# A hybrid DiT layer on one core: output projection by half token tiles, first MLP block in two halves, second norm without POOL, two hidden parts stored as hi and lo

## The chip, the core and the metric

The kernel runs on one core of one Trainium2 chip. A core has TensorE (PE: matrix products and transposes into the PSUM banks; its weight loads are shown as PEld), VectorE (DVE), ScalarE (ACT), GpSimd (POOL), SyncE (SP, which here only issues transfers), and transfer queues (DMA) between DRAM and the on-chip memory SBUF. Each engine works through its own instructions in order and waits on semaphores for the others. The metric is the device time of one execution in microseconds.

## The reference

One layer of a diffusion backbone on 1024 latent and 128 context tokens, `D_MODEL` 1024, everything in float32. What matters here is its second half:

```python
mix = (sigmoid(ga) * attn + sigmoid(gc) * conv) @ w_o
x = layer_norm(ALPHA * x + g1 * mix, ln1_g, ln1_b)
h = x * (1 + sc2) + sh2
f = square(relu(h @ w1 + b1)) @ w2 + b2
x = layer_norm(ALPHA * x + g2 * f, ln2_g, ln2_b)
```

`w_o` is 1024 x 1024, `w1` 1024 x 4096, `w2` 4096 x 1024. Shift, scale and gate (`sh2`, `sc2`, `g1`, `g2`) are rows, one set for the latent and one for the context tokens. Before that come the input projections, neighbourhood attention and a short convolution; the change leaves them alone.

## The kernel before

**Precision.** A float32 operand is cut into hi (a cast to the matrix format, on ACT) and lo (the difference, on DVE), and each product is three matmuls: hi x hi, hi x lo, lo x hi. So each operand costs one ACT cast and one DVE subtraction before PE can use it.

**Tokens** are 1152 columns: nine tiles of 128, three chunks of 384, or, for the MLP, two pairs of 576 (each two halves of `PT` = 288). Tile 4 lies across the two pairs.

**Order.** The program is written out by hand. Within one engine the order is that of the calls. `bg` is a list of small closures; `background(n)` (L705) calls the next n of them between groups of matmuls.

**Weights** of the projections come through `Ring` (L66 to L132): `load_to` issues the transfer of a 128 x 1024 raw tile (2 buffers) on SP, `split_hi` casts on ACT (L108), `split_lo` subtracts on DVE (L121) into one of 3 pairs of buffers; `take` returns the next pair and splits some ahead.

**Output projection** (L1150 to L1177). For each of three chunks, all eight 128-row blocks of `w_o` are streamed through the ring again (24 tiles of 512 KB). For each block, three token tiles accumulate into two PSUM banks each (`token_mm`, L990; six matmuls of 512 columns). At the end of a chunk `ln1_first` (L968) multiplies by the gate row (L974) and adds the residual (L975) for a whole tile; closures then take the moments (L981, L962 to L965), apply the norm on ACT (L985) and write the normalized tile to DRAM (`xd`, on ACT's queue, L986).

**Turning and modulating.** Normalized tiles are transposed on PE (L1043, L1058) and modulated by ACT on the way out of PSUM (L1033). For pair 0 `raw_four` does four tiles at once (512 columns), for pair 1 384 + 128. Pair 0 is done in the background of chunk 2; pair 1 after the projection has ended (L1189).

**First MLP product** (L1239 to L1319). It is a seven-product (Strassen-like) scheme over 16 blocks `j`: seven combinations of quarters of the tokens' matrix (`combine`, L1063: subtractions L1084, casts L1075, low parts L1079) meet seven combinations of quarters of `w1` (`w1_sum`, `w1_prep`, L1112 to L1146). `w1_mm` does both pairs, 24 matmuls of 288 columns for each of the seven. Results are kept on ACT (L1247) and added on DVE (L1250), then passed through relu and square, combined into seven hidden parts `B11 T1 T2 B21 T3 B22 T4` and written to DRAM as float32 (`spill`, L1235, on ACT's queue).

**Second MLP product** (L1590 to L1650). It runs through 7 products; the first five take both pairs in one step (24 matmuls, 80 steps), the last two (with `T4` and `B21`) one pair at a time (12 matmuls, 64 steps). `f2_load` (L1357) brings the weights and the hidden part seven steps ahead, `f2_prep` (L1388) cuts them three steps ahead (L1396 on ACT, L1399 on DVE).

**Second norm** (`ln2`, L1464) runs tile by tile (96 tokens) in the gaps of the last two products, from the list `side` with a credit per step (L1648). `residual` multiplies x by `ALPHA * ln1_g` on POOL (L1478), `o1` and `o2` transpose the result back and add it (L1486, L1491, L1492), `apply` normalizes on ACT (L1500), `gain` multiplies by a row on POOL (L1504), `last` adds a row on DVE (L1508). The last three tiles are ended by `end` (L1511) with work on ACT, POOL and DVE.

Of the kernel before, what the change touches and what calls it, by code (L numbers as in the profile page):

```python
# [18 lines left out]
P = 128  # L19
D = 1024  # L20
# [46 lines left out]
class Ring:  # L67
# [20 lines left out]
    def load_to(self, n):  # L88
        n = min(n, len(self.seq), self.nlo + self.raw_bufs + (1 if self.more else 0))
        while self.nload < n:  # L90
            ap, w = self.seq[self.nload]
            t = self.tile(F32, "wraw", self.nload, self.raw_bufs, "r")
            self.nc.sync.dma_start(t[:, :w], ap)
            self.raw[self.nload] = t
            self.nload += 1
# [48 lines left out]
def emit(nc, tc, ctx, aps, outs):  # L144
# [43 lines left out]
    for c in range(NCH):  # L188
        seq += [(aps["wo"][k], 1024) for k in range(KB)]
# [746 lines left out]
    sx0, sraw, sln, sw = ExitStack(), ExitStack(), ExitStack(), ExitStack()  # L936
    wsp = pool_on(sw, "wsp", side="right")
    hx0 = pool_on(sx0, "hx0", side="right")
    rawp = pool_on(sraw, "rawp", side="right")
# [13 lines left out]
    grow = [row(lnp, f"g{cond}", modd[cond, 0:D]) for cond in range(2)]  # L953
    xks = {}

    def load_xk(t):
        xks[t] = lnp.tile([P, D], F32, name=f"xk{t}")
        dma(xks[t], aps["xk"][t])
# [9 lines left out]
    def ln1_first(t, ps):  # L968

        x = xks[t]  # L970
        r = tmp(lnp, [P, D], "lnt", 1)
        g = grow[1 if t == 8 else 0]
        for i in range(2):
            vec.tensor_tensor(out=r[:, HALVES[i]], in0=ps[i], in1=g[:, HALVES[i]], op=ALU.mult)  # L974
        vec.scalar_tensor_tensor(out=x, in0=x, scalar=ALPHA, in1=r, op0=ALU.mult, op1=ALU.add)  # L975
        m = tmp(const, [P, 4], "bag", 6)

        def stats():
            s_ = tmp(const, [P, 2, 6], "bst", 3)
            for i in range(2):  # L980
                vec.bn_stats(out=s_[:, i], in_=x[:, HALVES[i]])  # L981
            moments(m, s_)

        def apply():
            act(x, x, AF.Identity, scale=m[:, 2:3], bias=m[:, 3:4])  # L985
            nc.scalar.dma_start(xd[t], x)  # L986

        return [stats, apply]

    def token_mm(banks, a, i, w, first, last, kb):  # L990

        ts_ = slice(i * P, (i + 1) * P)
        ah, al = a[0][:, kb, ts_], a[1][:, kb, ts_]
        for half in range(2):
            mm(banks[half], lhsT=ah, rhs=w[0][:, HALVES[half]], start=first, stop=False)
            mm(banks[half], lhsT=ah, rhs=w[1][:, HALVES[half]], start=False, stop=False)
        for half in range(2):
            mm(banks[half], lhsT=al, rhs=w[0][:, HALVES[half]], start=False, stop=last)  # L998
# [21 lines left out]
    def place(pair, store):  # L1020
        for name in PARTS:
            hx[pair][name] = (next(store), next(store))
# [714 lines left out]
```

## Time and profile before

| | |
|---|---|
| time, median of 3 runs | 1725.75 us (1725.08 to 1726.24) |
| profiled execution, its own time | 1729.52 us |
| its span | 1727.7 us |
| PE busy | 1615.9 us (94%) |
| DVE busy | 1065.2 us (62%) |
| ACT busy | 739.2 us (43%) |
| POOL busy | 230.7 us (13%) |
| mean granted PE clock | 0.974 |
| DMA | 223.56 MB, mean 129 GB/s |

Busy time of PE counts overlapping matmuls once, and a matmul that runs at half clock is busy for longer; so 94% does not mean that 6% is all there is to win. The rows below that matter are those that cut the span into stretches: in each, the busy time of each engine with its number of instructions, then the granted clock of PE (1.00 is full), the busy share of the 16 DMA engines and the GB/s that they moved. A row of waits reads: who waited, for whom, in total, how many times, the longest.

### The profile page before, as it was taken

Reading aid. Unit: us, or ns where it says so; the run is one execution under the profiler, and the core shown is the slowest. Engines: PE = TensorE matmul, PEld = TensorE weight load, DVE = VectorE, ACT = ScalarE, POOL = GpSimd, SP = SyncE. Lnnn points to the kernel's source line nnn. Section 1 sums busy time; section 2 is a strip of 40 time slices with the busy share of each in tenths; the row PEclk is TensorE's granted clock in tenths of the full one; section 3 lists DMA queues with packets and bytes.
Section 4 is the critical chain, followed back from the end, with each engine's and each line's share of the span. In section 5 each row is a group of like instructions: output and inputs, shape, how many; then the busy total and the mean of one; then the engine's idle time right before and its main releaser. Section 6 shows DMA issues by size and latency. Waiting matters only on the chain. (4 is left out here: it accounts for less than half of the span.)

```text
span 1727.7 us, 27190 instructions
## 1 busy us (share of the span) xinstructions
PE 1615.9 (94%) x10432; PEld 1549.5 (90%) x10432; DVE 1065.2 (62%) x1799; ACT 739.2 (43%) x1368; POOL 230.7 (13%) x226
## 2 busy tenths in 40 slices
PE   8999999999999999998765999999999999997794
PEld 5799999999999999986555999999999999997784
DVE  6468888654455555245575555555555668677777
ACT  5367777421111211233346555555554444543441
POOL 2145555000000012110000000000000000013323
PEclk9999999999999999999887999999999999999897
DMA  8331211222322133134411333443448866773542
GB/s 318 129 103 52 70 46 47 86 95 86 107 86 68 54 107 80 62 110 170 167 53 52 138 133 131 141 145 136 143 153 273 260 207 205 249 226 102 158 145 81
DMA packets 125241, 223.56 MB, mean 129 GB/s; under 512 B 38784, under 2 KB 48640, under 8 KB 125112
## 3 DMA queue, kind: packets, MB, share of 16 engines
q1 hardware_dynamic: 107544, 184.07, 33.7%
q10 hardware_dynamic: 17568, 37.76, 6.0%
q8 instruction: 82, 1.34, 0.3%
q14 instruction: 47, 0.39, 0.1%
HBM read 176.39 MB, written 45.38 MB: 128 GB/s over the span
## 5 line engine op out<-in xcount | busy, mean ns | idle before, releaser
L363 PE MATMUL ps<-ahi,wl 128*128 128x384 f32 x864 | 292.7, 339 | 0.0
L359 PE MATMUL ps<-ahi,wh 128*128 128x384 f32 x864 | 292.7, 339 | 0.0
L361 PE MATMUL ps<-alo,wh 128*128 128x384 f32 x864 | 292.7, 339 | 0.0
L1432 PE MATMUL pq<-xh,vh 128*128 128x288 f32 x640 | 189.6, 296 | 0.9 <-ACT vh L1420 0.9
L1433 PE MATMUL pq<-xl,vh 128*128 128x288 f32 x640 | 188.9, 295 | 0.0
L1434 PE MATMUL pq<-xh,vl 128*128 128x288 f32 x640 | 188.3, 294 | 0.2 <-DVE vl L1422 0.2
L1399 DVE TENSOR_TENSOR xl<-hraw,xh 128x576 fp32r<-128x576 f32 (+1 forms) x144 | 109.8, 765 | 105.4 <-ACT xh L1396 105.4
L359 PEld LDWEIGHTS ps<-ahi,wh 128*128 128x128 f32 x864 | 162.4, 188 | 1.5
L361 PEld LDWEIGHTS ps<-alo,wh 128*128 128x128 f32 x864 | 162.5, 188 | 0.8
L363 PEld LDWEIGHTS ps<-ahi,wl 128*128 128x128 f32 x864 | 162.4, 188 | 0.0
L1396 ACT CAST xh<-hraw 128x576 fp32r<-128x576 f32 (+1 forms) x144 | 79.7, 564 | 167.4 <-issue 91.7
L121 DVE TENSOR_TENSOR wl<-wr,wh 128x1024 fp32r<-128x1024 f32 (+1 forms) x69 | 79.5, 1155 | 111.3 <-ACT wh L108 111.1
L1478 POOL TENSOR_TENSOR x<-x,ag 96x1024 f32<-96x1024 f32 x12 | 31.6, 2638 | 778.3 <-DMA x<-xd 778.3
L1432 PEld LDWEIGHTS pq<-xh,vh 128*128 128x128 f32 x640 | 119.9, 187 | 1.2 <-ACT vh L1420 1.1
L1434 PEld LDWEIGHTS pq<-xh,vl 128*128 128x128 f32 x640 | 120.5, 188 | 0.4 <-DVE vl L1422 0.4
L1433 PEld LDWEIGHTS pq<-xl,vh 128*128 128x128 f32 x640 | 120.2, 188 | 0.1
L739 DVE SCALAR_TENSOR_TENSOR acc<-wmb,sil,acc 128x512 f32<-128x512 f32 x112 | 81.7, 772 | 28.6 <-DMA wmb<-wmb 28.4
L108 ACT CAST wh<-wr 128x1024 fp32r<-128x1024 f32 (+1 forms) x77 | 73.6, 968 | 51.9 <-PE ps L998 22.2
L1433 PE MATMUL pq<-xl,vhA 128*128 128x288 f32 x256 | 80.6, 315 | 14.8 <-DVE xl L1399 14.7
L1432 PE MATMUL pq<-xh,vhA 128*128 128x288 f32 x256 | 81.5, 318 | 9.0 <-DVE accc L1542 7.0
L1221 PE MATMUL dX<-hxahi,w1whi 128*128 128x288 f32 x256 | 77.1, 301 | 9.1 <-ACT c L1247 5.9
L1434 PE MATMUL pq<-xh,vlA 128*128 128x288 f32 x256 | 79.0, 309 | 2.4 <-DVE vlA L1422 2.4
(302 smaller groups left out, 4258.2 us busy)
## 6 DMA issues: line engine op xcount, KB each, us to landing
w2r<-w SPq DMA_DIRECT2D x144, 256.0 KB
wmb<-wmb SPq DMA_DIRECT2D x64, 256.0 KB
w1r<-w SPq DMA_DIRECT2D x32, 512.0 KB
hdB<-h ACTq DMA_DIRECT2D x48, 288.0 KB
hdT<-hT ACTq DMA_DIRECT2D x48, 288.0 KB
hraw<-hdT SPq DMA_DIRECT2D x48, 288.0 KB
wr<-wo SPq DMA_DIRECT2D x24, 512.0 KB
hraw<-hdB SPq DMA_DIRECT2D x32, 288.0 KB
```

Of the source, the lines that this page charges most:

```text
L108: self.nc.scalar.copy(hi[:, :w], self.raw[i][:, :w])
L121: engine.tensor_tensor(out=lo[:, :w], in0=self.raw.pop(i)[:, :w], in1=hi.bitcast(F32)[:, :w], op=ALU.subtract)
L359: mm(b[:, :CH], lhsT=hi[:, ws], rhs=a[0][:, kb, :], start=first and kb == 0, stop=False)
L361: mm(b[:, :CH], lhsT=hi[:, ws], rhs=a[1][:, kb, :], start=False, stop=False)
L363: mm(b[:, :CH], lhsT=lo[:, ws], rhs=a[0][:, kb, :], start=False, stop=last and kb == n - 1)
L739: vec.scalar_tensor_tensor(out=a, in0=t, scalar=sil[:, k, cond:cond + 1], in1=a, op0=ALU.mult, op1=ALU.add)
L1221: mm(o, lhsT=hi[:, ws], rhs=xh, start=first and kb == 0, stop=False, **kw)
L1396: nc.scalar.copy(xh[:, :np_], x[:, :np_])
L1399: vec.tensor_tensor(out=xl[:, :np_], in0=x[:, :np_], in1=f32(xh)[:, :np_], op=ALU.subtract)
L1432: mm(o, lhsT=hi[:, ws], rhs=xh[:, i], start=j == 0, stop=False)
L1433: mm(o, lhsT=hi[:, ws], rhs=xl[:, i], start=False, stop=False)
L1434: mm(o, lhsT=lo[:, ws], rhs=xh[:, i], start=False, stop=j == NJ - 1)
```

## The change

Four things are done together; the diff is cut to its core.

1. *Output projection.* `w_o` is taken by halves of its columns. All eight blocks of one half are resident (four ring tiles of two blocks each, three in the ring and a fourth in a new pool), and half token tiles go through one after the other in three passes: half 0 of tiles 0 to 5, half 1 of tiles 0 to 8, half 0 of tiles 6 to 8. Each half tile has one bank and 24 matmuls. The norm follows tile by tile. The work between is given out by `spend`, with a budget in microseconds per k-block. The background also prepares the parts of `w1` for blocks 0 and 1 (`w1_ahead`) and keeps them in DRAM; `w1_prep` fetches them. x tiles are written to DRAM on SP's queue.

```diff
-    for c in range(NCH):
-        seq += [(aps["wo"][k], 1024) for k in range(KB)]
+    for half in (0, 1, 0):
+        seq += [(aps["wo"][k:k + 2, :, half * 512:half * 512 + 512].rearrange("k p c -> p k c"), 1024)
+                for k in range(0, KB, 2)]
...
+    def ln1_sum(t, half, ps, g, seen):
+        x = xks[t, half]
+        r = tmp(lnp, [P, 512], "lnt", 1)
+        vec.tensor_tensor(out=r, in0=ps, in1=g, op=ALU.mult)
         vec.scalar_tensor_tensor(out=x, in0=x, scalar=ALPHA, in1=r, op0=ALU.mult, op1=ALU.add)
+        vec.bn_stats(out=seen[t][:, half], in_=x)
...
+    PASSES = ((0, range(6)), (1, range(9)), (0, range(6, 9)))
...
+    def spend(us):
+        room[0] = min(room[0] + us, 1.5)
+        while todo and (room[0] >= 0 or not todo[0][0]) or spare and room[0] >= 0:
+            cost, fn = (todo or spare).popleft()
+            fn()
+            room[0] -= cost
...
+    for ps, (half, ts_) in enumerate(PASSES):
+        w = [ring.take(ahead=0) for _ in range(4)]
+        for t in ts_:
+            b = bank(4 + (sums + 2) % 4)
+            spill_x()
+            next_xk()
+            for kb in range(KB):
+                wh, wl = (x[:, HALVES[kb % 2]] for x in w[kb // 2])
+                mm(b, lhsT=ah[:, kb, cols], rhs=wh, start=kb == 0, stop=False)
+                mm(b, lhsT=ah[:, kb, cols], rhs=wl, start=False, stop=False)
+                mm(b, lhsT=al[:, kb, cols], rhs=wh, start=False, stop=kb == KB - 1)
+                if t == ts_[-1] and kb % 2:
+                    if ps == 2:
+                        if kb < 7:
+                            w1_prep(kb - 1)
+                            w1_prep(kb)
+                    else:
+                        ring.split_to(ring.nuse + kb // 2 + 1)
+                        ring.load_to(len(seq))
+                        room[0] -= 1.2
+                spend(0.69)
+            first = [(2.05, lambda t=t, half=half, b=b, g=g: ln1_sum(t, half, b, g, seen))]
+            if ps == 2 or ps == 1 and t < 6:
+                first.append((0.9, lambda t=t: ln1_apply(t, seen)))
+            todo.extendleft(reversed(first))
+            if ps == 1 and 1 <= t < 6:
+                put_turn(t - 1, 0)
```

2. *First MLP block, pair by pair.* `turn` transposes half a token tile as soon as it is normalized and modulates it in four pieces (eight for a tile that crosses the middle of a pair). Block 0 of the first product is done for pair 0 first, then for pair 1; the turns and combinations of pair 1 are given out between pair 0's seven products, and each product of pair 1 is preceded by the combination that it needs.

```diff
+            for i in range(4):
+                nc.tensor.transpose(b[:, i * P:(i + 1) * P], xks[t, half][:, i * P:(i + 1) * P], ident)
...
+            for i in range(4):
+                kb = 4 * half + i
+                for x, y, n in pieces:
+                    act(raw[pair][half][x // PT][:, i, x % PT:x % PT + n], b[:, i * P + y:i * P + y + n], AF.Identity,
...
+        for pairs in ((0,), (1,)) if j == 0 else ((0, 1),):
...
+                while pairs == (1,) and made <= k:
+                    todo.popleft()[1]()
+                w1_mm(b, u + k, PARTS[k], bool(new), pairs)
...
+                if pairs == (0,):
+                    if k == 0:
+                        w1_prep(6)
+                        w1_prep(7)
+                    spend(1.6)
```

3. *Two hidden parts as hi and lo.* `B21` and `T4` are cut where they are made, in the first product, and written as two arrays; the last two products load both and cut nothing.

```diff
+            def parts(name, t):
+                hi = tmp(hip, [P, 2, PT], "hi" + name, 1, F32R)
+                nc.scalar.copy(hi, t)
+                vec.tensor_tensor(out=t.bitcast(F32R), in0=t, in1=f32(hi), op=ALU.subtract)
+                late.append(lambda: (nc.scalar.dma_start(hd[name, j][:, :, 0], f32(hi)),
+                                     nc.scalar.dma_start(hd[name, j][:, :, 1], t)))
...
-            dma(x[:, 0], hd[hn, j][:, pairs[0]])
+            x = tmp(fp, [P, 2, PT], ("hraw", "xh", "xl")[(n - 5 * NJ) // 4 % 3], 4, F32R)
+            dma(f32(x), hd[hn, j][:, pairs[0]])
...
+        if two:
+            xh, xl = x[:, 0:1], x[:, 1:2]
```

4. *Second norm without POOL.* The product with `ALPHA * ln1_g` is done once per x tile in DRAM during the first products (`scale_x`: load, POOL, store; every third step from the ninth to the thirty-third). `gain` and `last` become one DVE operation each that take in the mean and the reciprocal deviation; `apply` and `residual` go. `end` of the last three tiles stays, but is issued one tile earlier. The credits of the steps are raised, and the early split of the sixth product's weights starts four steps later.

```diff
+    def scale_x(t):
+        x = tmp(xmp, [P, D], "xm", 4)
+        dma(x, xd[t])
+        pl.tensor_tensor(out=x, in0=x, in1=ag, op=ALU.mult)
+        scaled.extend([lambda: None, lambda: None, lambda: nc.scalar.dma_start(xd[t], x)])
...
         def gain():
-            r = q["x"][:TT]
-            pl.tensor_tensor(out=r, in0=r, in1=rows2["g"][:TT], op=ALU.mult)
+            r, m = q["x"][:TT], q["m"]
+            vec.scalar_tensor_tensor(out=r, in0=r, scalar=m[:TT, 0:1], in1=rows2["g"][:TT], op0=ALU.subtract,
+                                     op1=ALU.mult)
...
-        credit = min(credit + (1.0 if not two else 0.4 if q == 6 and pairs == (0,) else 1.1), 1.5)
+        credit = min(credit + (1.0 if not two else 0.8 if q == 6 and pairs == (0,) else 1.45), 1.5)
```

More of the change, by code (lines that the diff above doesn't have):

```diff
@@ L966, in moments, with ln1_apply, spill_x @@
                           op1=ALU.mult)
[L968 to L998, printed above, removed]
+    def ln1_sum(t, half, ps, g, seen):
+        x = xks[t, half]
+        r = tmp(lnp, [P, 512], "lnt", 1)
+        vec.tensor_tensor(out=r, in0=ps, in1=g, op=ALU.mult)
+        vec.scalar_tensor_tensor(out=x, in0=x, scalar=ALPHA, in1=r, op0=ALU.mult, op1=ALU.add)
+        if t not in seen:
+            seen[t] = tmp(const, [P, 2, 6], "bst", 6)
+        vec.bn_stats(out=seen[t][:, half], in_=x)
+    def ln1_apply(t, seen):
+        m = tmp(const, [P, 4], "bag", 2)
+        moments(m, seen.pop(t))
+        for half in range(2):
+            x = xks[t, half]
+            act(x, x, AF.Identity, scale=m[:, 2:3], bias=m[:, 3:4])
+        to_spill.append(t)
+    to_spill = deque()
+    def spill_x():
+        while to_spill:
+            t = to_spill.popleft()
+            for half in range(2):
+                dma(xd[t][:, HALVES[half]], xks[t, half])
     PT = 288
@@ new lines, in low @@
+        def low(name, src):
+            hi, lo = hx[pair][name]
+            if isinstance(lo, str):
+                lo = [(tmp(rawp, [P, 4, PT], lo, 1, F32R), 0, 4)]
+                hx[pair][name] = hi, lo
+            step = min(n for _, _, n in hi + lo)
+            for k in range(0, 4, step):
+                (h_, hk), (l_, lk) = (next((x, k0) for x, k0, n in y if k0 <= k < k0 + n) for y in (hi, lo))
+                vec.tensor_tensor(out=l_[:, k - lk:k - lk + step], in0=src[:, k:k + step],
+                                  in1=f32(h_)[:, k - hk:k - hk + step], op=ALU.subtract)
@@ new lines, in w1_prep, with wo_last, next_xk @@
+        if k == 6 and j + 1 >= AHEAD:
+            w1_load(j + 1)
+    def wo_last(n):
+        return [wop.tile([P, 1024], F32R, tag=t, name=f"{t}{n}", bufs=1) for t in ("wh3", "wl3")]
+    PASSES = ((0, range(6)), (1, range(9)), (0, range(6, 9)))
+    order_xk = [(t, half) for half, ts_ in PASSES for t in ts_]
+    n_xk = [0]
+    def next_xk():
+        if n_xk[0] < len(order_xk):
+            load_xk(*order_xk[n_xk[0]])
+            n_xk[0] += 1
+    for _ in range(3):
+        next_xk()
+    seen, sums = {}, 0
@@ new lines, in emit, with put_turn @@
+    todo, spare = deque(), deque()
+    room = [0.0]
+    def spend(us):
[4 more added lines that the diff above has]
+            room[0] -= cost
+    turn_banks.extend(lambda i=i: bank(i) for i in range(4))
+    def put_turn(t, pair):
+        todo.extend((0.4, turn(t, pair, half)) for half in range(2))
+    for j in range(AHEAD):
+        spare.extend(w1_ahead(j))
@@ L1523, in end @@
             dma(outs["y"][t0:t0 + TT, a], r[:TT, a])
[L1525 removed]
+        return {"end": end, "load": load, "o1": back(0), "o2": back(1), "stats": stats,
                 "gain": gain, "last": last}
```

465 lines of the change are left out of this document (244 added, 221 removed).

## The prediction

> **What bounds the kernel now.** I read the totals first, then stretches cut where TensorE (PE) changes its work, then PE's waits in the bad ones.
>
> ```profile
> span 1727.7 us, 27190 instructions
> ```
> ```profile
> core 0: us, PE busy (x) PEld busy (x) DVE busy (x) ACT busy (x) POOL busy (x), PEclk, DMA share, GB/s
> 758.80:899.60 140.80, 116.68 (x475) 90.40 (x473) 76.86 (x98) 50.11 (x62) 1.56 (x2) 0.92 0.43 149
> 899.60:960.10 60.50, 35.23 (x208) 33.26 (x209) 35.29 (x51) 34.41 (x59) 0.00 (x0) 0.77 0.14 51
> 960.10:1295.20 335.10, 335.10 (x2520) 335.10 (x2519) 187.09 (x282) 176.81 (x283) 0.00 (x0) 1.00 0.41 142
> ...
> 1346.00:1398.00 52.00, 52.00 (x392) 52.00 (x391) 32.01 (x49) 22.24 (x43) 0.00 (x0) 1.00 0.74 230
> 1398.00:1551.60 153.60, 153.60 (x1154) 153.60 (x1153) 115.44 (x178) 75.38 (x134) 8.28 (x3) 1.00 0.73 230
> 1551.60:1705.30 153.70, 127.20 (x859) 121.17 (x858) 119.15 (x179) 54.91 (x115) 44.21 (x18) 0.92 0.45 130
> 1637.00:1665.00 28.00, 27.89 (x191) 27.88 (x191) 20.21 (x39) 15.68 (x33) 0.00 (x0) 0.89 0.69 207
> 1705.30:1727.70 22.40, 3.06 (x21) 2.10 (x19) 16.34 (x25) 3.00 (x6) 9.54 (x6) 0.64 0.18 53
> ```
>
> Call them **A** output projection, **B** block 0 of the first MLP product with what precedes it, **C** blocks 1 to 15, **D** the first five second-MLP products (to 1551.6), **E** the last two, **F** the end. C and D are full: 2520 matmuls of 288 columns in 335.1 us are 0.133 us each at clock 1.00, so PE bounds them and nothing can be won. A, B and E hold the loss: PE waits, and the clock falls below 1.
>
> ```profile
> PE ps L1043 <- ACT xk L985: 14.8, 3, 11.9
> PE ps L995 <- ACT wh L108: 8.1, 3, 4.6
> ```
> ```profile
> PE pq L1433 <- DVE xl L1399: 14.7, 11, 2.0
> PE pq L1432 <- DVE accc L1542: 7.0, 2, 4.8
> ```
>
> (Total, times, longest; first fence A and B, second E.) In A, PE waits for weight splits and for normalized tiles that it must transpose (and at the start of B for the same tiles). In E it waits for the split of the spilled hidden parts. A stall is paid twice:
>
> ```profile
> 777.00 0.50 PE L995 MATMUL ps<-wh,ahi 128*128 128x512 f32 x1 [1.68 <-ACT wh L108]
> 778.26 0.51 PE L996 MATMUL ps<-wl,ahi 128*128 128x512 f32 x1 [0.76 <-DVE wl L121]
> ```
> ```profile
> 779.50:783.00 3.50, 3.50 (x10) 2.75 (x9) 0.00 (x0) 1.04 (x1) 0.00 (x0) 0.51 0.71 277
> ```
>
> 2.4 us of idleness are followed by 3.5 us at clock 0.51: another 1.7 us. The Trainium skill, page "TensorE: Matmul & The Clock Gate", section "Why this matters for your kernels", says that the clock drops after gaps of more than about 3 us; here two gaps of 1.68 and 0.76 did it, so the trace speaks against that rule, and the sum goes by the row.
>
> **Part 1, output projection (A).** It still has 432 matmuls of 512 columns.
>
> ```profile
> 789.73 0.39 PE L995 MATMUL ps<-wh,ahi 128*128 128x512 f32 x1
> ...
> 791.09 0.39 PE L995 MATMUL ps<-wh,ahi 128*128 128x512 f32 x1
> ```
> ```profile
> 761.37 1.05 ACT L108 CAST wh<-wr 128x1024 fp32r<-128x1024 f32 x1
> ```
> ```profile
> 764.07 2.35 DVE L121 TENSOR_TENSOR wl<-wr,wh 128x1024 fp32r<-128x1024 f32 x2
> ```
> ```profile
> 1645.62 0.44 PE pq L1486 x4
> ```
> ```profile
> L1143 DVE TENSOR_TENSOR w1wlo<-S,w1whi 128x512 fp32r<-128x512 f32 x64 | 44.0, 688 | 35.4 <-ACT w1whi L1142 35.2
> ```
>
> Six matmuls in 1.36 us: 432 take 97.9. Ten turns (four transposes, 0.44) of pair 0 lie inside: 4.4. A half tile now eats its four weight tiles in 5.4 us, where one lasted 4.1 before. Only two are split ahead. The third and fourth still get their low parts from the two subtractions at 764.07, behind the eight splits of the last mix chunk: the third is ready at 765.2, needed at 758.8 + 4 x 0.68 = 761.5. That is 3.7 of waiting and 1.7 of slow clock. At the two changes of pass the third tile's raw load goes out only after the first one's subtraction; split 1.05 + 1.2, load, split again are about 8 us against the 8.2 until its use. I bound the stall by 0 and 5 each and take 2. A is 97.9 + 4.4 + 5.4 + 4 = **111.7**, for 140.8: **-29.1**.
>
> DVE's work in A is 18 half-tile sums near 2 us, ten weight subtractions (1.2), 14 + 8 operations of 0.69 for W1 ahead and nine combination steps of 1.3, some 80 of 112: hidden, with four banks of slack. Transfers: 4.2 MB weights, 4.7 x, 1.0 gate rows, 2.1 W1, 7.3 W1 parts out, 3.1 back, 4.7 x out: 27 MB, 242 GB/s. The stage moved 149 at a share of 0.43, so 347 would fill it. SP now carries all of these in order, and waits there for DVE's low parts; behind them stand x loads, issued three tiles (16 us) ahead, and weight loads, which are the 0 to 5 above.
>
> **Part 2, block 0 pair by pair (B).** What moves is the start: PE has seven units (1.6 us each) of pair 0 while pair 1 is prepared. What does not shrink is ACT and DVE.
>
> ```profile
> 915.82 9.75 ACT L1033 ACTIVATE raw<-ps,m2col 128x384 f32<-128x384 f32 x24 [0.57 <-PE ps L1043]
> 925.33 1.28 ACT L1075 CAST hxahi<-raw 128x1152 fp32r<-128x1152 f32 x1
> ```
> ```profile
> 946.53 1.36 DVE L1079 TENSOR_TENSOR hxs<-t,hxs 128x1152 fp32r<-128x1152 f32 x1 [1.22 <-ACT hxs L1075]
> ```
> ```profile
> L974 DVE TENSOR_TENSOR lnt<-ps,g 128x512 f32<-128x512 f32 x18 | 11.6, 684 | 0.8 <-PE ps L998 0.5
> L975 DVE SCALAR_TENSOR_TENSOR xk<-xk,lnt 128x1024 f32<-128x1024 f32 x9 | 11.0, 1225 | 0.3
> L981 DVE BATCH_NORM_STATS2 bst<-xk 128x6 f32<-128x512 f32 x18 | 11.5, 680 | 0.0
> L985 ACT ACTIVATE xk<-xk,bag 128x1024 f32<-128x1024 f32 x9 | 11.1, 1231 | 0.8 <-ACT xk L985 0.8
> ```
> ```profile
> 911.93 0.21 DVE L962 BATCH_NORM_AGGREGATE bag<-bst 128x2 f32<-128x12 f32 x1
> ...
> 912.71 0.21 DVE L965 TENSOR_SCALAR bag<-bag 128x1 f32<-128x1 f32 x1
> ```
>
> I counted out the budget that the order code keeps (0.69 given per k-block; taken: 2.05 for a sum, 1.4 for a subtraction, 0.4 for a turn). Over the 18 half tiles it is used up: when the last tile ends, all ten turns of pair 1 (tiles 4 to 8, two halves) are still queued, and so is pair 0's last part. A turn modulates token tile by token tile, in pieces of 32 to 128 columns: tiles 4, 5, 7 and 8 take 8 ACT instructions each, tile 6, which crosses the half of the pair, 16. That is 48 where there were 24. The 24 took 0.41 each with 384 columns among them; I take 0.34 (bounds 0.30, 0.41): 16.3. From the last matmul, T: about 1 of leftover on DVE, the last sum 2 (0.68 + 0.61 + 0.68, half of 1.23 as the second), statistics 1.0 (911.93 to 912.92), apply 1.2, then pair 0's T3 cast and two copies out of PSUM, 1.8, bring ACT to the modulations at T + 7; with two more copies they end at T + 23.6. PE, meanwhile, waits for the four banks that the turns share. Then the chain of subtract, cast, subtract for seven parts, which took 925.33 to 947.9 = 22.6 and is the same eleven DVE steps: T + 46. The sixth and seventh units follow, 3.2 and slow clock 1.7: **T + 51**, for 60.5: **-9.5**. Bounds: 27 (PE's 22.4 and ten turns) and 60.
>
> C: block 1's W1 parts come from DRAM. Each block of 22.3 us gains two casts on ACT and two subtractions on DVE, of 576 columns, so half of the 1.28 and 1.36 above: 1.3 and 1.4 beside ACT 53% and DVE 56% busy. PE's full row hides them: nothing.
>
> **Part 3, two parts as hi and lo, no POOL in the second norm (D, E, F).**
>
> ```profile
> L1399 DVE TENSOR_TENSOR xl<-hraw,xh x61: 435/446/2436, 1555.4 to 1702.0; 128x288 fp32r<-128x288 f32 x61
> ```
> ```profile
> L1508 DVE TENSOR_TENSOR x<-x,ln2b 96x1024 f32<-96x1024 f32 x9 | 22.5, 2503 | 0.0
> ```
> ```profile
> 1681.12 2.59 POOL L1478 TENSOR_TENSOR x<-x,ag 96x1024 f32<-96x1024 f32 x1
> ```
>
> The subtraction takes 0.446 at the median and up to 2.44, which fits waiting out a POOL multiplication of 2.59; `last` takes 2.50 where 1.2 would do (L975, the same size). E loses its 64 subtractions, the 64 casts ahead of them and POOL; DVE adds nine scalar operations near 1.2, and `last` returns to 1.2: at most 119 - 27 (61 x 0.446, less than they cost) - 22.5 + 21.6 = 91 of 115. So nothing but PE bounds E: 768 x 0.133 = 102.1, 21 turns 9.2, and 4 for bank waits (7.0 now, longest 4.8) and transfers: **115.5**, for 153.7: **-38.2**.
>
> ```profile
> w2r<-w SPq DMA_DIRECT2D x144, 256.0 KB
> hraw<-hdB SPq DMA_DIRECT2D x32, 288.0 KB
> ```
>
> Transfers are late next. The first half of A12 loads 544 KB per 1.6 us step, with three x and three y tiles of 96 x 1024 words 11 MB in 28 us, 395 GB/s; 207 at share 0.69 means 300, so 37 us, 9 late, against a lead of four to seven steps (6.4 to 11.2). In D, x goes to POOL and back: 2 x 512 KB every third step; at 1346 to 1398 18.7 MB, 360 GB/s against 230/0.74 = 311: 8 late, lead four steps of 3.2. Its nine POOL multiplications meet DVE 62% busy. Bounds for D 0 and 8; I take **+2**. F: the six POOL operations of the last three tiles stay; the first tile's are issued ahead of the third's turn and statistics (0.7 + 0.7 + 1.0 sooner), the others as before: **-1** (bounds -2.4, +1).
>
> **Sum.** -29.1 - 9.5 + 2 - 38.2 - 1 = -75.8. The profiled run took 1729.52 (span plus 1.8), its span becomes 1652; the median shown, 1725.75, is 3.8 under the profiled run, and less 75.8 it gives **1650**.
>
> **Rivals.**
> - **Block 0 fully covered** (0.10): modulations and chain hide behind units. For it: the order code fills them in between. Against: 39 us of ACT and DVE in series. B 27: 1626.
> - **Transfers late, mildly** (0.16): D pays 8, the A12 half 9 with 1.7 of clock, each pass change 5 with clock: 1650 + 6 + 8 + 1.7 + 9.4 = 1675.
> - **POOL moved, not removed** (0.07): D's nine multiplications each cost PE 1.3 (14.7/11) and clock 1.7: 1675. For it: the same pair of operations stalled E. Against: steps of 3.2 us, three prepared ahead. The Trainium skill's page "SBUF — State Buffer" ("SBUF: two separate sides") says that DVE operations with two SBUF inputs and POOL lock one port pair for a whole instruction, whichever starts first; by that rule moving POOL spares DVE nothing, and the 2.44 above agrees.
> - **Short stalls do not slow the clock** (0.08): the 1.7s go, and some 1.5 of the pass changes: 1645. The row at 779.5 speaks against it. It is the result of the Trainium skill's rule on the clock gate, quoted above.
> - **Slower** (0.04): transfers run at the rates moved before: 27 MB at 149 GB/s make A 181 (+69), 18.7 MB at 230 the second product 81 (+29): 1748. With D's 29 paid, it decides once A moves less than 27/(111.7 + 47) = 170 GB/s. Against: 277 moved at 779.5 in this very stage.
>
> Forecast 0.55, itself 1636 to 1666. The range leaves out the first and last rivals (0.14) and a little more: 1630 to 1682. About 0.2% is what a measurement here can tell from no change: faster 0.96, same 0.01, slower 0.03.
>
> **What would show it.** A near 112 with one stall in the first half tile and short ones at the pass changes; B near 51, with PE waiting for the subtractions that are now L1079; no subtraction of hidden parts in the last two products; those near 115 at clock 0.97 or more; D still full. A wrong count of what is queued at T, or a share of DMA near 1 in A, would make it wrong.

## The result and the profile after

The changed kernel takes 1687.22 us (median of 4 runs, 1685.68 to 1689.34) where the kernel before, on the same chip, takes 1725.99 (1725.08 to 1726.92): a ratio of 0.9776, 95% interval 0.9759 to 0.9793. That is 38.8 us less, 2.2%. The forecast was 75.8 less; 1687 lies above the end of its range (1682). The sign and the tail were right, the two stages A and B were not.

The windows of the changed kernel, cut where PE changes its work as in the prediction (columns as there: stretch and length, busy time and instructions of PE, PE's weight loads, DVE, ACT, POOL, then granted clock, DMA share, GB/s):

```profile
758.00:886.80 128.80, 112.24 (x474) 87.89 (x472) 78.10 (x123) 54.69 (x104) 1.60 (x2) 0.95 0.53 177
886.80:952.90 66.10, 44.20 (x209) 39.94 (x209) 26.07 (x31) 36.26 (x78) 0.00 (x0) 0.72 0.39 136
952.90:1288.50 335.60, 335.60 (x2522) 335.60 (x2521) 205.75 (x308) 195.22 (x312) 0.00 (x0) 1.00 0.50 172
1288.50:1549.70 261.20, 256.72 (x1922) 256.01 (x1921) 172.51 (x271) 118.64 (x210) 22.33 (x9) 1.00 0.83 275
1549.70:1662.30 112.60, 112.37 (x854) 111.45 (x853) 74.25 (x122) 21.73 (x45) 0.00 (x0) 1.00 0.79 251
1662.30:1683.90 21.60, 2.45 (x13) 1.26 (x12) 15.21 (x25) 3.00 (x6) 9.30 (x6) 0.67 0.19 55
```

The stage D of the kernel before, of which the prediction shows only stretches:

```profile
1295.20:1551.60 256.40, 255.31 (x1911) 254.72 (x1910) 174.97 (x267) 118.96 (x212) 8.28 (x3) 1.00 0.75 239
```

Against the forecast, stage by stage:

| stage | before | forecast | after | off by |
|---|---|---|---|---|
| A, output projection | 140.8 | 111.7 | 128.8 | +17.1 |
| B, block 0 of the first MLP product | 60.5 | 51 | 66.1 | +15.1 |
| C, blocks 1 to 15 | 335.1 | 335.1 | 335.6 | +0.5 |
| D, first five second products | 256.4 | 258.4 | 261.2 | +2.8 |
| E, last two second products | 153.7 | 115.5 | 112.6 | -2.9 |
| F, end | 22.4 | 21.4 | 21.6 | +0.2 |

E gains what it was to gain. A gains 12 instead of 29, and B, which was to gain 9.5, loses 5.6. PE's waits in A and B together (total, times, longest):

```profile
PE ps L1252 <- DVE wl L122: 8.7, 5, 4.1
PE dWturn L1051 <- ACT q L1061: 5.7, 2, 3.5
PE dX L1312 <- ACT q L1061: 4.2, 2, 2.1
PE ps L1251 <- ACT wh L109: 3.6, 5, 1.5
...
PE ps L1051 <- ACT xk L997: 2.6, 2, 1.8
```

The split of the output projection's weights (`wh`, `wl`) is still what A waits for most, 12.3 us in these two rows. In B PE waits for ACT's modulations `q`, both from turns (`dWturn`) and from units (`dX`; a unit is one of the seven products of block 0 for one pair). In E there is no wait left but this one:

```profile
PE pq L1616 <- DVE accc L1671: 0.3, 1, 0.3
```

**A, the two changes of pass** (timeline: start, duration, engine, line; the bracket is the idle time before and its releaser):

```profile
796.35 0.62 ACT L1158 CAST ehT<-eh 128x512 fp32r<-128x512 f32 x1 [6.64 <-DMA eh<-w]
796.88 1.99 ACT L109 CAST wh<-wr 128x1024 fp32r<-128x1024 f32 x2
797.97 0.49 PE L1251 MATMUL ps<-wh,ahi 128*128 128x512 f32 x1 [1.49 <-ACT wh L109]
799.23 0.80 PE L1252 MATMUL ps<-wl,ahi 128*128 128x512 f32 x1 [0.76 <-DVE wl L122]
799.82 0.63 PE L1253 MATMUL ps<-wh,alo 128*128 128x512 f32 x1
802.78 1.05 ACT L109 CAST wh<-wr 128x1024 fp32r<-128x1024 f32 x1 [3.92 <-DMA wr<-wo]
...
860.96 1.99 ACT L109 CAST wh<-wr 128x1024 fp32r<-128x1024 f32 x2
...
863.30 0.69 DVE L985 TENSOR_TENSOR lnt<-ps,g 128x512 f32<-128x512 f32 x1
...
865.36 2.34 DVE L122 TENSOR_TENSOR wl<-wr,wh 128x1024 fp32r<-128x1024 f32 x2
866.62 0.80 PE L1252 MATMUL ps<-wl,ahi 128*128 128x512 f32 x1 [4.08 <-DVE wl L122]
```

At the first change ACT stood 6.64 us at the cast of W1's second block, which is made ahead and has until block 1 begins, because its load had not landed. The cast of the weights that PE needs at once stood behind it. Then the third weights came late in their own right: ACT waited 3.92 us for their load. The matmul after the waits takes 0.63 us, not 0.39. At the second change the casts themselves come late, behind a backlog of modulations and combine casts, and DVE makes combine low parts and a half tile's sums (from 863.30) before the low parts that PE waits 4.08 us for.

**B** (timeline):

```profile
896.26 1.29 ACT L1061 ACTIVATE q<-dX,m2col 128x64 f32<-128x64 f32 x4
897.60 0.40 PE L1312 MATMUL dX<-hxahi,w1whi 128*128 128x288 f32 x1 [2.07 <-ACT q L1061]
...
900.54 0.50 ACT L1363 ACTIVATE c<-dX,b1c 128x288 f32<-128x288 f32 x1 [2.99 <-PE dX L1314]
...
902.56 1.51 ACT L1061 ACTIVATE q<-dWturn,m2col 128x128 f32<-128x128 f32 x4
...
904.13 0.66 PE L1051 MATMUL dWturn<-ident,xk 128*128 128x128 f32 x4 [2.23 <-ACT q L1061]
...
908.35 0.46 DVE L1366 TENSOR_TENSOR h<-dZ,c 128x288 f32<-128x288 f32 x1 [11.50 <-PE dZ L1314]
...
922.38 1.16 ACT L1069 CAST hxahi<-q 128x1152 fp32r<-128x1152 f32 x1
```

PE and ACT take turns at waiting: a unit waits for a modulation, ACT's copy of that unit's sum (L1363) stands ahead of the next modulations and waits for the unit, the next turn waits for them. DVE sits idle for 11.5 us, and pair 1's first combine cast comes at 922.38, that is 35.6 us after the last matmul of A.

### The profile page after: what moved, and what is told of

The parts are those of the page before. It is cut to its first block, busy times and chain, and to the rows that moved or that the text cites. A ratio compares the mean times of both kernels' runs of the same rounds, so it can differ in the third digit from the quotient of the medians.

```text
span 1683.9 us, 27308 instructions
## 1 busy us (share of the span) xinstructions
PE 1605.1 (95%) x10432; PEld 1543.4 (92%) x10432; DVE 1027.2 (61%) x1777; ACT 730.4 (43%) x1384; POOL 200.2 (12%) x214
## 4 chain that ended last, share of the span: by engine, by line
PE 77%; DVE 9%; ACT 6%; issue 3%; DMA 3%; POOL 0%; SPq 0%; POOLq 0%; ACTq 0%; DVEq 0%
PE ps L363 8%; PE ps L365 8%; PE ps L361 8%; PE pq L1565 6%; PE pq L1566 6%; PE pq L1567 6%; PE dX L1312 3%; PE dX L1314 3%; PE dX L1313 3%; PE ps L813 2%; PE ps L812 2%; PE ps L811 2%; PE dV L1313 2%; PE dV L1312 2%; PE dV L1314 2%
## 5 line engine op out<-in xcount | busy, mean ns | idle before, releaser
L1532 DVE TENSOR_TENSOR xl<-hraw,xh 128x576 fp32r<-128x576 f32 x80 | 60.5, 756 | 78.3 <-ACT xh L1528 78.2
L122 DVE TENSOR_TENSOR wl<-wr,wh 128x1024 fp32r<-128x1024 f32 (+1 forms) x54 | 61.2, 1137 | 62.9 <-ACT wh L109 62.8
L1713 POOL TENSOR_TENSOR xm<-xm,ag 128x1024 f32<-128x1024 f32 x9 | 22.3, 2481 | 625.9 <-DMA xm<-xd 587.6
L1528 ACT CAST xh<-hraw 128x576 fp32r<-128x576 f32 x80 | 53.9, 673 | 97.5 <-issue 40.8
L1314 PE MATMUL dX<-hxahi,w1wlo 128*128 128x288 f32 x248 | 74.1, 299 | 0.1
L563 ACT ACTIVATE s<-s,st 128x512 f32<-128x512 f32 (+1 forms) x72 | 49.6, 688 | 51.5 <-DVE st L561 50.9
L1363 ACT ACTIVATE c<-dX,b1c 128x576 f32<-128x576 f32 (+1 forms) x51 | 36.4, 713 | 74.7 <-PE dX L1314 70.5
L109 ACT CAST wh<-wr 128x1024 fp32r<-128x1024 f32 (+1 forms) x62 | 57.7, 949 | 20.0 <-DMA wr<-wo 11.4
```

The source lines that it names most:

```text
L122: engine.tensor_tensor(out=lo[:, :w], in0=self.raw.pop(i)[:, :w], in1=hi.bitcast(F32)[:, :w], op=ALU.subtract)
L1314: mm(o, lhsT=lo[:, ws], rhs=xh, start=False, stop=kb == 3, **kw)
L1532: vec.tensor_tensor(out=xl, in0=f32(x), in1=f32(xh), op=ALU.subtract)
```

## The experiments

Stage times below are windows cut at the same places of each kernel's own profile.

**The tail alone: the kernel before with the third part of the change** (the parts `B21` and `T4` kept as hi and lo, their loads, the second norm and the scaling taken over from the changed kernel):

```
 def f2_load(n):
...
-        x = tmp(fp, [P, 2, PT], "hraw", 4)
         if two:
-            dma(x[:, 0], hd[hn, j][:, pairs[0]])
+            x = tmp(fp, [P, 2, PT], ("hraw", "xh", "xl")[(n - 5 * NJ) // 4 % 3], 4, F32R)
+            dma(f32(x), hd[hn, j][:, pairs[0]])
```

> The kernel before with the third part alone (two parts kept as hi and lo, no POOL in the second norm). If the stages of the changed kernel do not act on each other: output projection and block 0 as before (140.8 and 60.5 us), the first five second products 261, the last two 112.6, the end 21.6, in all 1726 - 37 = 1689 us, so that the first two parts together are worth only some 2 us. Rival: the new output projection's order shapes what follows; then the last two products differ from 112.6 by more than 3 us, or the first five from 261 by more than 2.

Measured: 1690.95 us, ratio 0.9786 (0.9763 to 0.9809). A and B took 140.7 and 60.3, the last two products 111.8, the first five 260.8. These four differ by less than 1 us from what was expected, so the tail and the stages ahead of it do not act on each other. The tail gives all but some 4 us of the gain (1690.95 against 1687.22; the intervals of the two ratios overlap); the first two parts as written give 12 us in A and take 6 back in B.

**Turns first.** All ten turns of pair 1 ahead of unit 0:

```
                 turn_banks.extend(lambda n=n, i=i: B[n][:, i] for n, i in (("X", 1), ("V", 1), ("W", 0), ("W", 1)))
+                while todo[0][1] is not second_pair:
+                    todo.popleft()[1]()
```

> The changed kernel with all ten turns of pair 1 issued ahead of unit 0 of block 0, instead of four behind each unit. If units and turns hold each other up (PE in order, waiting in turn for ACT's 48 modulations, and ACT for PE), the modulations now run without gaps, some 18 us instead of 26, the first combine subtraction starts some 8 us sooner, the units fill the chain, and block 0 takes 66 - 12 = 50 to 56 us. If the sheer amount of ACT and DVE work in series sets it, block 0 stays at 63 or more, since PE's units now start 15 us later and nothing gets less.

Measured: 1677.22 us, ratio 0.9708 (0.9679 to 0.9736), block 0 53.0 us. Its window, and its PE and ACT waits there:

```profile
887.40:940.40 53.00, 33.77 (x210) 31.71 (x209) 25.69 (x31) 34.34 (x77) 0.00 (x0) 0.74 0.44 154
```
```profile
PE dWturn L1051 <- ACT q L1061: 16.1, 2, 11.1
```
```profile
ACT c L1363 <- PE dX L1314: 4.0, 2, 2.0
```

The changed kernel's ACT has this row in its place:

```profile
ACT c L1363 <- PE dX L1314: 12.7, 5, 4.2
```

PE waits longer in sum at the turns (16.1 us) and yet the stage is 13 us shorter: ACT's wait for units fell from 12.7 to 4.0 us, the modulations now run from 896 to 914, where they ran from 896 to 922. ACT does the same 48 modulations in both. So their amount is not what cost the time; the order was. The kernel is 10 us shorter, not 13: A took 129.5 and D 263.5 in this profile.

**Half of the modulations on DVE**, order as in the changed kernel:

```
                 for x, y, n in pieces:
+                    if pair and i > 1:
+                        vec.tensor_scalar(out=raw[pair][half][x // PT][:, i, x % PT:x % PT + n],
+                                          in0=b[:, i * P + y:i * P + y + n],
+                                          scalar1=m2col[:, cond, 1, kb:kb + 1], scalar2=m2col[:, cond, 0, kb:kb + 1],
+                                          op0=ALU.mult, op1=ALU.add)
+                        continue
```

> The changed kernel with half of pair 1's modulations (k-blocks 2 and 3 of each turn) on DVE, which stands idle for 23 us there. Amount of ACT work: 24 fewer at 0.38 us, so ACT is done 9 us sooner and block 0 takes about 57 us, the kernel 1678. Alternation of PE and ACT: each turn's bank comes free after 0.8 us instead of 1.5, units start sooner too, block 0 about 54, the kernel 1675. If the late transfers of block 0's W1 parts set it: no change, 66.

Measured: 1685.69 us (0.9758, 0.9736 to 0.9779), block 0 64.7: both theories that had half the work help by 9 us or more missed. The third, that the late transfers of W1's parts set block 0, is nearest in number, but turns first left the transfers as they are and gained 13 us. The reason stands in ACT's waits:

```profile
ACT c L1368 <- PE dX L1319: 13.5, 5, 4.6
ACT q L1066 <- PE dWturn L1051: 4.2, 3, 2.0
```

ACT has half the modulations and waits for PE instead. With PE and ACT in lockstep, less work for one of them is more waiting for it.

**Turn banks apart from the units' banks:**

```
-                turn_banks.extend(lambda n=n, i=i: B[n][:, i] for n, i in (("X", 1), ("V", 1), ("W", 0), ("W", 1)))
+                turn_banks.extend(lambda n=n, i=i: B[n][:, i] for n, i in (("W", 0), ("W", 1)))
```

> The changed kernel with the turns of pair 1 on the two banks of W alone, instead of the second banks of X and V and both of W; the order of the instructions stays. If the units wait because a turn's bank is the other half of their own two-bank tile (waits of 2.07, 2.14 and 1.59 us ahead of units 2, 4 and 5), these waits go, and block 0 takes 66 - 6 = 60 us or less. If PE's order does it (a turn that must wait for its bank holds the units behind it), two banks for ten turns make the waits longer, they only move from the units to the turns, and block 0 takes 66 to 74.

Measured: 1690.12 us (0.9781, 0.9753 to 0.9809), block 0 67.1. The units no longer wait for `q`, the turns do:

```profile
PE dWturn L1051 <- ACT q L1061: 10.7, 7, 2.6
```

So the shared tile is not what mainly held the units; the order in which PE and ACT alternate remains. Ten turns now have two banks instead of four, which lengthens their waits by itself, so a small part of the shared tile is not excluded.

**One block of W1 ahead instead of two, and no scaling of x** (this kernel leaves out the first norm's gain):

```
-    AHEAD = 2
+    AHEAD = 1
...
-        if 8 <= n < 35 and n % 3 == 0:
+        if False:
```

> The changed kernel with W1 parts made ahead for block 0 alone (not block 1), and without the scaling of x by the first norm's gain in the second product (its loads, POOL multiplications and stores are left out). Output projection: if ACT's and DVE's in-order work for block 1 (a cast that waited 6.6 us for its load) delays the weight splits, the stalls at the first change of pass (4.9 us and slow clock) fall under 1.5 and the stage to 121 to 124 us from 128.8; if the two raw weight buffers set it, the stalls stay near 5 and the stage over 127. First five second products: if the scaling's transfers cost the 4.8 us, 256.4; if the later splits of A22 do, 261 stays.

Measured: 1669.05 us (0.966, 0.9634 to 0.9686). Output projection and first five second products:

```profile
758.90:879.50 120.60, 111.60 (x475) 88.54 (x473) 73.80 (x114) 51.92 (x97) 1.57 (x2) 0.94 0.49 163
...
1276.50:1533.40 256.90, 256.30 (x1923) 256.06 (x1922) 170.40 (x271) 118.46 (x210) 0.00 (x0) 1.00 0.76 244
```

The second block costs A 8.2 us; B, too, is 4.6 shorter (61.5), and its unit 0 no longer waits 2.56 us for W1's parts. D is without its surplus. Waits of 2.5 us at the first and 3.4 us at the second change of pass were left, so the rival, the raw buffers, was not out.

**A third raw buffer**, for the third weights of the second and third pass, with one block ahead:

```
-        self.given = {}
+        self.given, self.graw = {}, {}
...
-        n = min(n, len(self.seq), self.nlo + self.raw_bufs + (1 if self.more else 0))
+        n = min(n, len(self.seq), self.nlo + self.raw_bufs + (1 if self.more else 0)
+                + sum(self.nlo <= i < self.nlo + self.raw_bufs + 1 for i in self.graw))
...
-            t = self.tile(F32, "wraw", self.nload, self.raw_bufs, "r")
+            t = self.graw[self.nload]() if self.nload in self.graw else self.tile(F32, "wraw", self.nload, self.raw_bufs, "r")
...
+    for p in (1, 2):
+        ring.graw[ring.nuse + 4 * p + 2] = lambda p=p: lnp.tile([P, 1024], F32, tag="wr3", name=f"wr3{p}", bufs=1)
```

> The changed kernel with W1 parts ahead for block 0 alone, and a third raw buffer for the third weights of the second and third pass (the scaling by the gain is as in the changed kernel again). The output projection took 119.9 us with one block ahead, with 2.5 us of waits at the first and 3.4 at the second change of pass. If the third weights' late load sets these, both fall under 1 us and the stage to 115 or 116; if the order of casts and subtractions or the split buffers do, it stays at 119 to 121. The first five second products are to be at 261 again if the scaling costs the 4.4 us that went without it.

Measured: 1672.87 us (0.9681, 0.9644 to 0.9718).

```profile
758.40:874.90 116.50, 109.01 (x475) 86.98 (x474) 73.55 (x114) 51.85 (x97) 1.58 (x2) 0.97 0.50 169
...
1272.20:1540.70 268.50, 260.99 (x1923) 260.28 (x1922) 176.40 (x272) 119.43 (x211) 21.59 (x9) 0.98 0.81 269
```

A lost another 4.1 us, about what was expected, but the waits did not both fall under 1 us: the first change of pass has 0.59, 0.56 and 0.75 us now, the second keeps its 1.74 and 0.76. D, with the scaling back, took 268.5: more than the 261 expected. The profile is of the longer of two runs (1676.6 and 1669.14 us), so the scaling's price is not steady; in the profiles of six kernels that have it, all but the two experiments below, D took 260.8 to 268.5 us.

**The gain on DVE in the second norm, no pass through DRAM:**

```
                     q["m"] = tmp(lp, [P, 4], "bag2", 6)
+                    vec.tensor_tensor(out=q["x"][:TT], in0=q["x"][:TT], in1=rows2["ag"][:TT], op=ALU.mult)
...
-        if 8 <= n < 35 and n % 3 == 0:
-            scale_x(n // 3 - 3)
```

> The changed kernel without the scaling pass through DRAM: the first norm's gain is multiplied in by DVE when the second norm first touches a tile, 12 multiplications of 96x1024 near 1.2 us in the last two products, where DVE is busy 74 of 113 us. If the 9.4 MB of x to and fro delay the weights of the second product, its first five products fall from 261.2 to 256.8, and the last two stay at 112 to 114, since DVE has 38 us to spare: kernel 1683. Rival: DVE's order delays the transposes there, the last two products go to 117 or more, and the kernel gains nothing.

Measured: 1682.93 us (0.974, 0.9718 to 0.9762).

```profile
1288.90:1545.80 256.90, 256.30 (x1923) 256.07 (x1922) 170.54 (x271) 118.65 (x210) 0.00 (x0) 1.00 0.76 243
1545.80:1658.10 112.30, 112.07 (x852) 111.26 (x852) 86.17 (x132) 21.73 (x45) 0.00 (x0) 1.00 0.79 251
```

D is back at 256.9 and E stays at 112.3 with 12 us more of DVE: the first of the two theories holds for the scaling pass as a whole. The edit takes POOL's multiplications away with the transfers, so the next two runs part them.

**The scaling's two halves, each alone.** First the transfers without the multiplication, then the multiplication without transfers (both leave out the gain itself):

```
         dma(x, xd[t])
-        pl.tensor_tensor(out=x, in0=x, in1=ag, op=ALU.mult)
         scaled.extend([lambda: None, lambda: None, lambda: nc.scalar.dma_start(xd[t], x)])
```

> The changed kernel with x loaded and stored in the second product as before, but not multiplied (the gain is left out). If the transfers delay the weights, the first five second products stay at 261 or more; if POOL's multiplications hold up DVE, they fall to 257.

```
-        dma(x, xd[t])
-        pl.tensor_tensor(out=x, in0=x, in1=ag, op=ALU.mult)
-        scaled.extend([lambda: None, lambda: None, lambda: nc.scalar.dma_start(xd[t], x)])
+        pl.tensor_tensor(out=x, in0=ag, in1=ag, op=ALU.mult)
```

> The opposite: the nine POOL multiplications run, on a resident row, and nothing of x is loaded or stored (x stays without its gain). Transfers theory: 257. POOL theory (ports shared with DVE): 261 or more.

Measured: D 261.9 and 265.3 (kernels 1685.14 and 1689.94). The first row is the transfers, the second POOL:

```profile
1289.10:1551.00 261.90, 258.29 (x1922) 257.58 (x1921) 170.39 (x271) 118.76 (x210) 0.00 (x0) 0.99 0.83 275
```
```profile
1289.50:1554.80 265.30, 258.81 (x1922) 257.57 (x1921) 184.83 (x271) 118.96 (x211) 20.56 (x9) 0.99 0.74 236
```

Each half alone costs D 5 to 8 us, but the second run did more than part them. With no tile of x to wait for, POOL made all nine multiplications in one stretch (POOL and DVE in that run):

```profile
1320.93 20.56 POOL L1712 TENSOR_TENSOR xm<-ag 128x1024 f32<-128x1024 f32 x9 [560.56 <-ACT ag L1727]
```
```profile
1323.36 2.38 DVE L1555 TENSOR_TENSOR vl<-w2r,vh 128x512 fp32r<-128x512 f32 x1
```

In the changed kernel they start 9 to 12 us apart, from 1324.71 to 1406.01, since each needs a tile of x that has to land first. In the stretch, nine DVE instructions of about 0.7 us took 2.0 to 2.4 each, which makes up the 14.3 us that DVE's 271 instructions take longer than without the scaling (184.83 instead of 170.54), and PE waited three times 1.21 us for DVE's low parts. The Trainium skill's rule on the port pair, weighed in the prediction (page "SBUF — State Buffer", section "SBUF: two separate sides"), agrees with these rows. In the changed kernel DVE took only 2 us longer (172.51), and no PE wait in D is for those low parts. So the second run shows what nine multiplications in a row cost, not what they cost the changed kernel. There, as in the run with transfers alone, PE waits where a product ends; this is the longer of the changed kernel's two such waits, with what held ACT up ahead of it:

```profile
1343.14 0.40 PE L1565 MATMUL pq<-xh,vh 128*128 128x288 f32 x1 [2.40 <-ACT accc L1661]
```
```profile
ACT xh L1528 <- DMA w2r<-w: 30.0, 6, 7.0
```

ACT's casts of the hidden parts wait 30 us in all for loads (the profile names those of the weights), the longest 7.04 us just before this copy, and the copies of the finished sums out of PSUM (`accc`) stand behind them on ACT. The waits are 2.40 and 1.49 us, together 3.9 of the 4.3 us that D is longer than without the scaling; with transfers alone they are 0.50 and 2.51, and without the scaling there are none. So in the changed kernel it is the transfers. That the multiplications add nothing to them rests on single profiles (261.2 with both, 261.9 with transfers alone).

**All edits together** (turns first, half of the modulations on DVE, one block ahead, third raw buffer, gain on DVE; the diffs are those above):

> All together: turns first, half of the modulations on DVE, one block of W1 ahead, the third raw buffer, the gain on DVE. With DVE taking half, the turns-first block should lose another 9 us, as ACT is then what PE waits for: block 0 in 44 to 47 us (53.7 with turns first alone). Output projection 116, first five products 257, last two 113: 1687 - 12 - 21 - 4 = 1650 us. If the combine chain behind the last tile sets block 0 (apply at T + 9, then 25 us and the last units), block 0 stays at 50 or more and the kernel at 1656.

Measured: 1652.69 us (0.9563, 0.9545 to 0.9581): A 116.0, B 48.4, D 257.4, E 112.4. The kernel came out 2.7 us above the expected 1650, since B missed its 44 to 47. B lost 4.6 us against turns first alone (53.0), where 9 were expected from DVE's half; one block of W1 ahead, which had shortened B by itself, stands between the two as well, so how much of the 4.6 is DVE's is not shown. After the modulations ACT stood idle 3.3 us at the copy of unit 0, with the first combine cast behind it; the next runs go at that.

**Pair 1's first combine steps ahead of unit 0**, once with the low parts of the last mix chunk on POOL, once with no background work in a pass's last tile, once alone:

```
                 while todo[0][1] is not second_pair:
                     todo.popleft()[1]()
+                for _ in range(5):
+                    todo.popleft()[1]()
```
```
+                pl.tensor_tensor(out=mc[1][:, j], in0=mix[j][:, csl(c)], in1=f32(mc[0][:, j]), op=ALU.subtract)
```
```
-                spend(0.69)
+                if not (ps < 2 and t == ts_[-1]):
+                    spend(0.69)
```

(The first piece is in all three; the second in the one with POOL, for the last chunk; the third in the one with the pause.)

> The best so far (1652.7 us) with two more edits. The first two combine steps of pair 1 come ahead of unit 0, so that ACT's cast does not stand behind the copy of unit 0: ACT was idle 3.3 us there, and the chain starts 4 us sooner; block 0 from 49.0 to 45. The low parts of the last mix chunk go to POOL, so that the third and fourth weights' low parts stand no longer behind eight subtractions on DVE: the first half tile's stall of 2.4 us and its slow clock of 1.7 go, output projection from 115.4 to 111.5. In all 1645 us. Rival: POOL's subtractions hold DVE's up, or the fourth weights come no sooner, since their cast stands behind ACT's eight casts; then the output projection stays at 115.

> The best so far with the first two combine steps ahead of unit 0, and with nothing taken from the queue of background work during the last tile of the first and second pass, when the next weights are split. If the queue's casts and subtractions cause what is left at the second change of pass (waits of 1.74, 0.76 and 1.32 us), these fall below 1.5 in all and the output projection from 115.4 to 113; more is left at its end, so block 0 45 to 47. In all 1647 us. Rival: the waits stay, because the split buffers come free too late; 115 and 47: 1650.

> The first version with all edits (1652.7 us) with pair 1's first combine steps ahead of unit 0, and nothing else. If ACT's copy of unit 0 holds the chain, block 0 goes from 49.0 to 46 or 47 (46.5 where another edit stood beside it) and the kernel to 1650. If the chain is set elsewhere, 49 and 1652.7.

Measured with POOL's low parts: 1657.23 (0.959, 0.9577 to 0.9604), A 122.2, B 45.8. The first half tile's waits did shrink, from 3.1 to 1.8 us, but the stage got 6 longer. POOL holds the mix tiles until 770, and what is loaded into their room next waits on SP; behind those loads stands W1's block, and ACT's first cast of it waits longer for its load than in the version without this edit (the first row of each fence is SP's wait for the mix tiles, the second ACT's for the load; version with POOL first):

```profile
SPq L959 <- POOL alo L935: 9.6, 1, 9.6
...
ACT ehT L1168 <- DMA eh<-w: 18.8, 1, 18.8
```
```profile
SPq L955 <- DVE alo L205: 4.8, 1, 4.8
...
ACT ehT L1164 <- DMA eh<-w: 12.2, 1, 12.2
```

While ACT stands there DVE stands behind it, no sums are made, and PE waits 3.09 us for a bank, and 4.23 at the first change of pass for low parts: a third case of background work in front of urgent work.

Measured with the pause: 1653.86 (0.9567, 0.9554 to 0.958), A 115.1, B 49.7. At the second change the waits of 1.75 and 0.76 us stayed and only a third, of 1.26, went. A is at the rival's 115, B above both forecasts. Measured alone: **1649.78** (0.9556, 0.9542 to 0.957), A 115.3, B 45.8 against 48.4 in the first version with all edits: the copy of unit 0 was what held the chain. Beside this run, the pause gave A 0.2 us and cost B 3.9, since more work was left at the end of A (DVE is busy for 38.4 us in B instead of 35.5). This is the fastest version, 37 us under the changed kernel and 76 under the kernel before as measured beside it (1725.7).

**Pair 0's combine after the second change of pass:**

```
         w = [ring.take(ahead=0) for _ in range(4)]
+        if ps == 2:
+            todo.append((0.0, lambda: todo.extendleft(reversed(combine(0)))))
+            put_turn(4, 1)
+            put_turn(5, 1)
```

> The same, with the whole combine of pair 0 (and the turns of tiles 4 and 5) queued only after the second change of pass. If the weights' casts stand behind a combine cast on ACT that waits for DVE, the waits of 1.75 and 0.76 us there go, the output projection falls from 115.4 to 112 or 113; but some 8 us of DVE work are moved behind, so block 0 goes to 52 to 54: 1655. If the split buffers set them, they stay, the output projection stays at 115, and block 0 still gets longer: 1658.

Measured: 1654.11 us (0.9577, 0.9563 to 0.9591). PE's waits in A of the fastest version, then of this one:

```profile
PE ps L1260 <- DVE wl L123: 4.4, 3, 2.4
PE ps L1259 <- ACT wh L110: 2.5, 2, 1.7
```
```profile
PE ps L1264 <- DVE wl L123: 2.4, 1, 2.4
...
PE ps L1263 <- ACT wh L110: 0.7, 1, 0.7
```

PE waits for nothing any more at the second change of pass (what is left in these rows is the first half tile's); A takes 111.0 us, B 54.0. It was ACT's queue: a combine cast that waits for DVE, with the weights' casts behind it. The pause had come too late for that cast: with and without it, ACT stood 3.76 us for DVE at the combine cast of 851.7, and the weights' casts came behind. And the price is as expected: the work moved out of A (the combine, and the turns of tiles 4 and 5) lengthens B by 8.2 us, more than A gained.

## Why the forecast was off

**Right.** E: 112.6 for 115.5; it is PE's, as argued, and the 4 us of waits and late transfers allowed there were 0.3. F: -0.8 for -1. C: hidden. So E's -38.2 measured -41.1. (The terms written down for E, 102.1, 9.2 and 4, add up to 115.3, not 115.5.) The rival "slower", at the rates moved before, fell: A moved 177 GB/s, D 275.

**A: the terms of the stall were mis-sized.** The first half tile (3.7 us of waiting forecast, 0.71 and 2.37 measured) stands. The step that failed is "I bound the stall by 0 and 5 each and take 2" at the changes of pass, and with it "DVE's work in A ... hidden, with four banks of slack". The waits were 4.9 us at the first change (1.49, 0.76, 0.36, 0.77, 1.52) and 5.9 at the second (0.85, 4.08, 0.22, 0.76), and at both changes matmuls at 0.63 stand behind the first waits. Another 2.6 us were waited ahead of two turns, for the norm on ACT, for which the sum has no term. In all PE waited 16.4 us in A, and with the slow clock and the slow first matmul behind each wait the 9.4 us that the sum has beside matmuls and turns became 26.5. The step priced background work by its busy time and took it as free wherever the sum fitted. What it costs is its place in the queue: ACT waited 18 us in all for loads of W1 that nobody needed yet, 6.64 of them in front of casts that PE needed at once, and DVE's low parts of the weights stood behind sums. The runs give the parts: 128.8 less 8.2 (second block), less 4.1 (raw buffer), less 4.3 (115.3 to 111.0, combine behind the change) is 112.2, and the run with all three, and the other edits, took 111.0, where the forecast had 111.7. So the forecast's A is about what this order takes once these three are out of the way; the third is not saved, but moved into B.

**B: the order failed, not the amounts.** The 48 modulations were priced at 16.3 us and took 16.7 of ACT's time (the rows of L1061: 6.1, 5.3, 5.3):

```profile
L1061 ACT ACTIVATE q<-dWturn,m2col 128x128 f32<-128x128 f32 x16 | 6.1, 474 | 2.0 <-PE dWturn L1051 2.0
L1061 ACT ACTIVATE q<-dX,m2col 128x64 f32<-128x64 f32 (+3 forms) x16 | 5.3, 442 | 0.0
L1061 ACT ACTIVATE q<-dV,m2col 128x64 f32<-128x64 f32 (+3 forms) x16 | 5.3, 422 | 0.9 <-PE dV L1051 0.7
```

The step that failed is that they would run from T + 7 to T + 23.6 (T = 886.8, the end of A): they ran from T + 9.5 to T + 35.6. "PE, meanwhile, waits for the four banks that the turns share" was seen as harmless; that the units' copies stand between the modulations on ACT, and so wait for PE, was not seen. The sum has 0.3 us for the two copies that stand there; they took 0.50 each and waited 2.99 and 3.34 for PE, and the modulations themselves waited another 2.7 for turns. The chain behind, priced 22.6 us, took 25 (922.4 to 947.5). Of the 15.1 us that B was off, the later start makes 2.5, the stretched modulations 9.5 and the chain 2.5. With turns first, B took 53.0; the forecast's 51 is near what the amounts give when nothing alternates.

**D.** Taken +2, bounds 0 and 8, measured +4.8: the right term, late transfers, sized too low. The rival "POOL moved" put a wait and slow clock on each of nine multiplications; the changed kernel has three waits of PE, 4.5 us together, none of them for DVE's low parts. What the rival describes is seen only in the POOL-only run, where the multiplications stand in a row.

**The rival nearest in number**, "transfers late, mildly" (1675), had 5 us at each change of pass right in size, but at the first change the loads were late by their place in SP's queue (W1's second block went out only at 791.94, behind stores that waited for ACT) and by two raw buffers, not by bandwidth: the DMA share in A was 0.53. The A12 half, which it had 9 late, waits for nothing. "Short stalls do not slow the clock" fell at the first waits of both changes of pass (0.63 us a matmul) and held for the waits behind them; "block 0 fully covered" fell with B at 66.1.

## What to carry to other kernels

Price background work by what stands behind it on an in-order engine, not by its busy time: a cast that waits for its own load, or a copy that waits for PE, holds every urgent instruction behind it, and the sum of busy times does not show it. Where two engines feed each other through few buffers, bring one kind of work to its end first, even if an engine then waits 16 us for it; halving one side's work in the alternation gave block 0 1.4 us, reordering gave it 13. When a change does several things at once, time the stages, not the kernel: here the tail alone gave nearly all of the gain, and mending the other stages gave 37 us, nearly as much again. And when an experiment takes one part of a pair away, look at whether what is left still runs at the same times: nine multiplications that no longer waited for their loads ran in one stretch and measured something else.

## What the hardware showed unasked

Small ACT instructions out of PSUM cost nearly the same between 64 and 128 columns: in B's timeline above, four of 64 columns take 1.29 us together, four of 128 take 1.51. DVE was hardly faster at the same pieces: in the kernel with half of the modulations on DVE, two of 128 columns took it 0.73 us together (at 904.04).

PE's clock after waits goes by more than the length of the last one. In the changed kernel, waits of 1.49 and 0.76 us were followed by matmuls of 512 columns at 0.63 us instead of 0.39, until 802.4; the next ones, 0.36, 0.77 and 1.52 us, from 803.5 to 808.3, were not: the matmuls behind them took 0.39 to 0.40. After the 16.1 us of waits in the turns-first run the first two units were slow (3.0 and 2.6 us from start to start), the third took 1.6. What decides is not shown by these runs.
